# Rooms for the weights' rests 4,224 bytes apart, and the moving parts of every product at one place modulo 256

## The chip, the cores and the metric

The kernel runs on one core of a Trainium2 chip. The metric is the device time of one execution in microseconds. Three runs of the kernel before took 1249.85 us at the median (1249.78 to 1250.2). The profile is one further execution of the same program.

## The reference

Two pre-norm residual layers over 512 tokens of width 1024, in float32. Layer 0 mixes tokens with a grouped complex diagonal state-space model (S5) and a GLU, layer 1 with forgetting attention (FoX, 16 heads of 64). Each is followed by a gated feed-forward with a causal depthwise convolution of width 3 (inner width 2816). A conditioning vector gives shift, scale and gate of every sub-layer. Cut to what the change touches:

```python
def modulate(x, g, shift, scale):
    return rmsnorm(x, g) * (1.0 + scale) + shift

def s5_mixer(h, w_in, ..., w_glu, w_out):
    u = h @ w_in
    ...                                    # scan over the tokens, gelu
    y = y * jax.nn.sigmoid(y @ w_glu)
    return y @ w_out

def fox_mixer(h, w_in, b_f, w_out):
    proj = h @ w_in                        # q, k, v and the forget logits
    ...
    return o @ w_out

def conv_ffn(h, w_up, conv_w, conv_b, w_down):
    a, b = jnp.split(h @ w_up, 2, axis=-1)
    ...                                    # causal convolution of a, width 3
    return (jax.nn.silu(a_conv) * b) @ w_down
```

## The kernel before, in words

**Products in three matmuls.** All activations lie transposed, channels on the 128 partitions and the 512 tokens along the free axis. A float32 weight tile is loaded (line 190, the tile `raw`) and split: ScalarE writes its rounded part `w_hi` (line 275), VectorE the rest `w_lo` = raw - w_hi (line 276). Activations are split in the same way: `a_hi` and `a_lo` for a normed input, `zhi`/`zlo` for the gated S5 output, `ghi`/`glo` for the gated inner layer, and the two halves `o[:, 0]`, `o[:, 1]` of the tile `v` for the attention output. For each of the 8 (or 5 or 6) slices of the contraction, `mms` (line 287) issues three matmuls on line 292: (`w_hi`, `x_hi`), (`w_hi`, `x_lo`), (`w_lo`, `x_hi`). The first of each pair is stationary (loaded by LDWEIGHTS), the second is the moving part, which streams 512 tokens of 4 bytes, or 256 in a half.

**Stages in order of time.** S5 runs up to 199 us with its float32 inputs and the first four columns of the GLU product (line 1190, `glu_head`); the rest of GLU and `w_out` follow up to 268. The first feed-forward (`ffn`, two groups of 11 inner tiles: up, down, up, down) runs up to about 650. Then come FoX: its values (line 1328, where the weights are the moving part and the input is stationary), the queries and keys with the attention worked in between (lines 1424, 1454, 1471), and `w_out` from about 836 to 893. The second feed-forward, with `plain` set, has four groups; most of its up product is formed from quarter matrices in seven products in place of eight (`quarters`, line 548; `forms_x` prepares the moving parts).

**Rings.** Weights live in the pool `wpool`: `raw` with 3 buffers, `w_hi` and `w_lo` with 5 each (`WB`). In the opening the three rings take turns for raw loads as well (`raw(..., n)`, line 185: n = 2 takes a `w_lo` buffer). The tile framework orders the instructions of each engine ahead of time and gives each new tile a buffer of its ring that has come free; a write waits for the last reader of the tile that had the buffer. In the program as built the buffers of `w_lo` are taken in one fixed turn.

**Places.** The free-axis addresses follow from the sizes of the pools. `a_hi` starts at byte 20,288 of each partition. `ROOM` enlarges the rooms of `a_hi` and `a_lo` by so many floats, and `WHOLE`, `HALF`, `PLAIN` say at which float the content starts (`normed`, line 130). `gap` (line 134) allocates a few floats that only shift what follows. `TAIL_OFF` and `DOWN_OFF` shift the weights inside wider rooms for the tail of a down product and for the other down products (line 628). Slices are 512 or 2,048 bytes, so a tile's place modulo 256 is the same for all its slices.

Of the kernel before, what the change touches and what calls it, by code (L numbers as in the profile page):

```python
# [8 lines left out]
F32 = mybir.dt.float32  # L9
F32R = mybir.dt.float32r  # L10
# [7 lines left out]
P = 128  # L18
D = 1024
KT = D // P  # L20
# [16 lines left out]
HALVES = (slice(0, S // 2), slice(S // 2, S))  # L37
RAW, WB = 3, 5

ROOM = {"a_hi": 112, "a_lo": 80}  # L40
WHOLE = {"a_hi": 0, "a_lo": 48}
HALF = {"a_hi": 112, "a_lo": 0}
PLAIN = {"a_lo": 16}
TAIL_ROOM = 7 * P
TAIL_OFF = {"w_hi": 80, "w_lo": 112}, {"w_hi": 96, "w_lo": 0}
DOWN_OFF = {"w_hi": 0, "w_lo": 96}

GROUPS = (11, 11)
QGROUPS = (6, 5, 6, 5)
# [14 lines left out]
class Trunk:  # L64
# [6 lines left out]
    def __init__(self, tc, io, ctx):  # L71
        self.tc, self.nc, self.io, self.ctx = tc, tc.nc, io, ctx
        nc = self.nc
        pool = lambda name, bufs, **k: ctx.enter_context(tc.tile_pool(name=name, bufs=bufs, **k))
        self.const = pool("const", 1)
        self.act = pool("act", 1)
        self.wpool = pool("wpool", 3)
        self.tmp = pool("tmp", 2)
        self.small = pool("small", 2)
        self.dram = pool("dram", 1, space=DRAM)  # L80
        self.mm = pool("mm", 4, space=PSUM)
        self.aux = pool("aux", 4, space=PSUM)
        self.bg = []
        self.acc = None
        self.pending = None
        self.spaced = False
# [12 lines left out]
        self.ga = [self.const.tile([P, KT], F32, name=f"ga{i}") for i in range(4)]  # L99
# [83 lines left out]
            yield  # L183

    def raw(self, shape, src, n=0):
        if n == 2 and not self.spaced:
            self.spaced = True
            self.gap(self.wpool, 32, "w_gap")
        t = self.wpool.tile(shape, F32, name="raw", tag=("raw", "w_hi", "w_lo")[n], bufs=(RAW, WB, WB)[n])
        self.nc.sync.dma_start(t, src)  # L190
        return t

    def ada_pe(self, i, thirds, late=False):

# [66 lines left out]
    def split(self, src, shape, pool=None, bufs=WB, off=None):  # L261

        if off:
            more = TAIL_ROOM - math.prod(shape[1:])
            hi, lo = (
                self.wide(pool or self.wpool, n, {"bufs": bufs}, F32R, more, off[n], shape) for n in ("w_hi", "w_lo")
            )
        else:
            hi, lo = ((pool or self.wpool).tile(shape, F32R, name=n, bufs=bufs) for n in ("w_hi", "w_lo"))
        self.put_parts(hi, lo, self.raw(shape, src))  # L270
        return hi, lo

# [20 lines left out]
                o, wt, xt[:, cols], start=(k == 0 and n == 0), stop=(k == nk - 1 and n == 2),  # L293
            )

    def product(self, w, ms, nk, x, evac, head=0, tail=0, after=None, ticks=0, halves=HALVES, tail_pool=(), first=None, step=None, apart=False, where=()):


        ms = list(ms)
        full = slice(0, S)  # L300
        if head:
            wk = first or {m: self.weights(w[m], nk) for m in ms[:head]}
# [9 lines left out]
                evac(m, ps[m], full)  # L312
                self.tick(ticks)
        for m in ms[head:len(ms) - tail]:
            wk = self.weights(w[m], nk, *where)
            ps = self.mm.tile([P, S], F32, name="mmp")
            for c in HALVES if apart else (full,):
                for k in range(nk):
                    self.mms(ps[:, c], wk, x, k, nk, c)
                    if step:  # L320
                        step()
            evac(m, ps, full)
            self.tick(ticks)
        if tail:
            last = ms[len(ms) - tail:]
# [184 lines left out]
    def quarters(self, pool, l, f, x, finish):  # L510

        nc = self.nc
        H, N = KT // 2, S // 2
# [5 lines left out]
        w = {}  # L519

        def parts(src, names, where=None):
            hi, lo = where or (
                self.wpool.tile([P, len(names) * H, P], F32R, name=n, bufs=WB) for n in ("w_hi", "w_lo")
            )
            self.put_parts(hi, lo, src)
            for j, n in enumerate(names):
                w[n] = hi[:, j * H:(j + 1) * H], lo[:, j * H:(j + 1) * H]
# [51 lines left out]
    def ffn(self, i, l, x, nxt, ticks=0, plain=None):  # L579

        nc, tc = self.nc, self.tc
        with tc.tile_pool(name=f"ffn{l}", bufs=1, reuse_waits="tile") as pool:
# [17 lines left out]
            def gated(m, ps, cols):  # L600
# [18 lines left out]
                self.put_parts(hi[:, j, :], lo[:, j, :], t)  # L619

            after, y = nxt
            up = lambda fs, **k: self.product(
                self.io["w_up"][l], range(2 * fs[0], 2 * fs[-1] + 2), KT, x, gated, ticks=ticks, **k
            )
            last = len(groups) - 1
            down = lambda q, ms, **k: self.product(
                self.io["w_down"][l][:, :, first[q]:first[q + 1], :], ms, groups[q], g[q],
                self.add_residual(i, q == last), after=after, ticks=ticks, where=(None, WB, DOWN_OFF), **k
            )
            todo = []  # L630
            for q, n in enumerate(groups):
# [146 lines left out]
class S5(Trunk):  # L778
# [291 lines left out]
    def s5(self, i, nxt):  # L1070
# [5 lines left out]
        with ExitStack() as stack:  # L1076
# [3 lines left out]
            with ExitStack() as start:  # L1080
# [12 lines left out]
                with tc.manual_schedule(engines={ENG.PE, ENG.Activation, ENG.DVE, ENG.SP}):  # L1093
# [18 lines left out]
                    rb = self.rms_rows(y, NB)  # L1112
                    next(params)
                    next(scale)
                    x = self.normed("a_lo", PLAIN, "a_x", F32)
                    for k in range(KT):
                        nc.vector.scalar_tensor_tensor(
                            x[:, k], self.h[:, k], self.ga[i][:, k:k + 1], rb, op0=ALU.mult, op1=ALU.mult
# [62 lines left out]
            def glu_head(k, part):  # L1181

                for m in range(HEAD):
                    if part and m not in lo:
                        lo[m] = self.wpool.tile([P, KT, P], F32R, name="w_lo", bufs=WB)
                        with tc.issue_after(self.scanned):
                            nc.vector.tensor_tensor(lo[m], raw[m], hi[m].bitcast(F32), ALU.subtract)
                    wt = (hi, lo)[part][m][:, k]
                    for xt in (yhi, ylo) if part == 0 else (yhi,):
                        nc.tensor.matmul(  # L1190
                            gps[m], wt, xt[:, k], start=(k == 0 and part == 0 and xt is yhi), stop=(k == KT - 1 and part == 1)
                        )
# [69 lines left out]
class Kernel(S5):  # L1262
# [320 lines left out]
```

## Time and profile before

| | before |
|---|---|
| median of three runs | 1249.85 us |
| the profiled execution's own time | 1250.39 us |
| its span, first to last instruction | 1248.6 us |
| TensorE busy with matmuls | 1225.7 us, 98% |
| VectorE, ScalarE, GpSimd busy | 896.8, 565.0, 57.6 us |
| mean granted TensorE clock | 0.994 |

The span and what lies around it (1.8 us) make the execution's own time, which is 0.54 us above the median of the runs. Matmuls are pipelined: the duration of one matmul overlaps the next, so a rate is read from how many matmuls a stretch of the chain holds and not from the duration of one. In a row of the chain of waits the first number is the start in us, the second the length in us, and "x174" the number of instructions that the row joins.

### The profile page before, as it was taken

Reading aid. Unit: us, or ns where it says so; the run is one execution under the profiler, and the core shown is the slowest. Engines: PE = TensorE matmul, PEld = TensorE weight load, DVE = VectorE, ACT = ScalarE, POOL = GpSimd, SP = SyncE. Lnnn points to the kernel's source line nnn. Section 1 sums busy time; section 2 is a strip of 40 time slices with the busy share of each in tenths; the row PEclk is TensorE's granted clock in tenths of the full one; section 3 lists DMA queues with packets and bytes.
Section 4 is the critical chain, followed back from the end, with each engine's and each line's share of the span. In section 5 each row is a group of like instructions: output and inputs, shape, how many; then the busy total and the mean of one; then the engine's idle time right before and its main releaser. Section 6 shows DMA issues by size and latency. Waiting matters only on the chain.

```text
span 1248.6 us, 19613 instructions
## 1 busy us (share of the span) xinstructions
PE 1225.7 (98%) x7584; PEld 1021.2 (82%) x7584; DVE 896.8 (72%) x1610; ACT 565.0 (45%) x1043; POOL 57.6 (5%) x111
## 2 busy tenths in 40 slices
PE   7999999999999999999999999999989999999997
PEld 2466677898778887787799888887989999999987
DVE  7888886479755546566457467765799978888865
ACT  3543455335333223333434366664456555555543
POOL 0000000000000000000000143331000000000000
PEclk9999999999999999999999999999999999999999
DMA  9678667336735746455423343240413332333331
GB/s 360 229 237 261 201 185 255 104 104 208 247 125 164 221 140 220 136 173 162 142 70 101 127 133 132 95 144 5 133 38 116 114 115 92 110 108 106 102 85 69
DMA packets 73068, 183.24 MB, mean 147 GB/s; under 512 B 23079, under 2 KB 25471, under 8 KB 71951
## 3 DMA queue, kind: packets, MB, share of 16 engines
q1 hardware_dynamic: 72687, 181.46, 45.0%
q8 instruction: 60, 0.98, 0.3%
q10 hardware_dynamic: 288, 0.52, 0.1%
q14 instruction: 33, 0.27, 0.1%
HBM read 175.04 MB, written 6.92 MB: 146 GB/s over the span
## 4 chain that ended last, share of the span: by engine, by line
PE 94%; DVE 3%; ACT 1%; DMA 1%; issue 1%; SPq 0%; DVEq 0%; ACTq 0%
PE mmp L292 57%; PE mmp L548 10%; PE mmp L1161 4%; PE aux L548 4%; PE mmp L1328 2%; PE aux L966 2%; PE mmp L1190 2%; PE aux L1471 2%; PE aux L1454 1%; PE mmp L209 1%; PE aux L1055 1%; PE aux L1047 1%; PE aux L1424 1%; PE mmp L1101 1%; PE aux L1005 1%; DVE w_lo L276 1%
## 5 line engine op out<-in xcount | busy, mean ns | idle before, releaser
L275 ACT ACTIVATE w_hi<-raw 128x1024 fp32r<-128x1024 f32 (+4 forms) x197 | 181.1, 926 | 257.5 <-PE mmp L292 211.0
L276 DVE TENSOR_TENSOR w_lo<-raw,w_hi 128x1024 fp32r<-128x1024 f32 (+4 forms) x197 | 210.1, 1068 | 90.4 <-ACT w_hi L275 86.1
L292 PE MATMUL mmp<-a_hi,w_hi 128*128 128x512 f32 (+1 forms) x664 | 244.3, 369 | 1.5 <-ACT a_hi L429 0.8
L292 PE MATMUL mmp<-a_hi,w_lo 128*128 128x512 f32 (+1 forms) x664 | 240.8, 363 | 3.1 <-DVE w_lo L276 3.1
L292 PE MATMUL mmp<-a_lo,w_hi 128*128 128x512 f32 (+1 forms) x664 | 241.6, 365 | 0.0
L292 PEld LDWEIGHTS mmp<-a_hi,w_hi 128*128 128x128 f32 x664 | 125.2, 189 | 25.7 <-issue 2.6
L292 PEld LDWEIGHTS mmp<-a_hi,w_lo 128*128 128x128 f32 x664 | 125.2, 189 | 24.5 <-DVE w_lo L276 3.3
L292 PE MATMUL mmp<-ghi,w_hi 128*128 128x512 f32 (+1 forms) x394 | 144.6, 367 | 0.0
L292 PE MATMUL mmp<-glo,w_hi 128*128 128x512 f32 (+1 forms) x394 | 144.1, 366 | 0.0
L292 PE MATMUL mmp<-ghi,w_lo 128*128 128x512 f32 (+1 forms) x394 | 144.0, 365 | 0.0
L292 PEld LDWEIGHTS mmp<-a_lo,w_hi 128*128 128x128 f32 x664 | 125.4, 189 | 18.6
L359 DVE SCALAR_TENSOR_TENSOR h<-mmp,par,h 128x512 f32<-128x512 f32 (+1 forms) x74 | 49.9, 676 | 58.0 <-PE mmp L292 57.7
L292 PEld LDWEIGHTS mmp<-ghi,w_lo 128*128 128x128 f32 x394 | 74.0, 188 | 12.2
L292 PEld LDWEIGHTS mmp<-ghi,w_hi 128*128 128x128 f32 x394 | 74.0, 188 | 11.6
L292 PEld LDWEIGHTS mmp<-glo,w_hi 128*128 128x128 f32 x394 | 74.0, 188 | 11.5
L237 DVE SCALAR_TENSOR_TENSOR ada_acc<-ada_raw,sc,ada_acc 128x1024 f32<-128x1024 f32 x49 | 62.8, 1282 | 27.9 <-DMA ada_raw<-in_ada_w 27.6
L548 PE MATMUL mmp<-w_hi 128*128 128x256 f32 x216 | 59.7, 277 | 0.0
L548 PE MATMUL mmp<-w_lo,w_hi 128*128 128x256 f32 x216 | 59.6, 276 | 0.0
L548 PE MATMUL mmp<-w_hi,w_lo 128*128 128x256 f32 x216 | 59.6, 276 | 0.0
L609 ACT ACTIVATE conv<-conv 128x512 f32<-128x512 f32 x44 | 27.6, 631 | 64.2 <-DVE conv L606 63.8
L1161 PE MATMUL mmp<-a_x,raw 128*128 128x512 f32 x112 | 56.2, 640 | 0.0
L276 DVE TENSOR_TENSOR w_lo<-sums,w_hi 128x1024 fp32r<-128x1024 f32 x40 | 48.5, 1221 | 3.3 <-ACT w_hi L275 2.1
(306 smaller groups left out, 2479.6 us busy)
## 6 DMA issues: line engine op xcount, KB each, us to landing
raw<-in_w_up SPq DMA_DIRECT2D x88, 512.0 KB, 3.3
ada_raw<-in_ada_w SPq DMA_DIRECT2D x56, 512.0 KB, 4.4
raw<-in_ada_w SPq DMA_DIRECT2D x40, 512.0 KB, 6.1
raw<-in_w_down SPq DMA_DIRECT2D x32, 384.0 KB, 3.2
raw<-in_w_down SPq DMA_DIRECT2D x32, 320.0 KB, 3.0
nf<-nfd SPq DMA_DIRECT2D x8, 1152.0 KB, 5.7
raw<-in_fox_qk SPq DMA_DIRECT2D x16, 512.0 KB, 3.6
h<-in_x SPq DMA_DIRECT2D x8, 512.0 KB, 5.2
```

Of the source, the lines that this page charges most:

```text
L237: nc.vector.scalar_tensor_tensor(acc, w, self.sc[:, k:k + 1], acc, op0=ALU.mult, op1=ALU.add)
L275: nc.scalar.activation(hi, src, AF.Copy)
L276: nc.vector.tensor_tensor(lo, src, hi.bitcast(F32), ALU.subtract)
L292: self.last_mm = self.nc.tensor.matmul(o, wt, xt[:, cols], start=(k == 0 and n == 0), stop=(k == nk - 1 and n == 2),)
L359: self.nc.vector.scalar_tensor_tensor(self.h[:, m, cols], ps, self.par[i][:, 16 + m:17 + m], self.h[:, m, cols], op0=ALU.mult, op1=ALU.add,)
L548: self.last_mm = nc.tensor.matmul(o, wt[:, k], xt[:, k], start=(first and k == 0 and n == 0), stop=(k == H - 1 and n == 2), skip_group_che ...
L609: nc.scalar.activation(t, t, AF.Silu)
L966: nc.tensor.matmul(ps[g2][:, j, cols], x[rows, a + j, r].rearrange("p c j -> p (c j)"), self.rr[rows, planes, q, :], start=(j == 0 and r = ...
L1161: nc.tensor.matmul(ps, w[m][:, k, :], x[:, k], start=(k == 0), stop=(k == KT - 1))
L1190: nc.tensor.matmul(gps[m], wt, xt[:, k], start=(k == 0 and part == 0 and xt is yhi), stop=(k == KT - 1 and part == 1))
L1328: self.last_mm = nc.tensor.matmul(ps[q, b][:, :n], xt[:, k, tb], wt, start=(k == 0 and i == 0), stop=(k == KT - 1 and i == 2),)
L1471: nc.tensor.matmul(pv[:, c * P:], self.v[:, hp, k, r].rearrange("p t d -> p (t d)"), pp[:, r, c + 3 * k:NB + 3 * k, :].rearrange("p b t -> ...
```

## The change

- `w_lo` is no longer one ring of five buffers. `rest` hands out five rooms, each a tag of its own with one buffer, in a fixed turn by a counter (`self.rests`). A room is 32 floats wider than the largest content, 4,224 bytes, so that the rooms start 0, 128, 0, 128, 0 bytes off modulo 256; the content starts 0 or 128 bytes in, by the room's number, or the other way round with `odd`. So all rests lie at one place modulo 256, and with `odd` all lie 128 bytes further.
- `odd` is set for the up products of the second feed-forward (`up` with `plain`, and `quarters`), not elsewhere. `DOWN_OFF` and `where` go, and with them the shifted rest of the down products; `w_gap`, which stood ahead of the `w_lo` ring, goes too.
- `ROOM`, `WHOLE`, `HALF` change, `PLAIN` goes; `zlo_gap` goes, and `v_gap` shrinks from 48 to 32 floats.

Worked out from the sizes: `a_hi` at 20,288 is 4,096 + 48 floats, so `a_lo` starts at 36,864 and is 4,096 + 16 floats; `wpool` starts at 53,312, `raw` and `w_hi` take eight times 4,096 bytes, and the rooms start at 86,080 and end at 107,200. The `w_lo` ring ended at 107,200 as well, so what follows in memory stays where it was, but for the tiles after the two changed gaps. Places modulo 256, in bytes:

| tile | before | after |
|---|---|---|
| `raw`, `w_hi` | 64 | 64 |
| `w_lo` and raw loads in its place | 192 | 64 |
| `w_lo` of the down products | 64 | 64 |
| `w_lo` of the second feed-forward's up products | 192 | 192 |
| `a_hi`, whole / for the second feed-forward | 64 / 0 | 64 / 0 |
| `a_lo`, whole / for the second feed-forward | 192 / 0 | 64 / 0 |
| `zhi`, `zlo` | 64, 192 | 64, 64 |
| `v` (and `o`), `phi`, `plo`, q and k parts | 128 | 64 |
| `ghi`, `glo` | 64 | 64 |
| weights of the down tails, hi / lo | 128 / 0 | 128 / 0 |
| moving parts of `quarters` | 0 | 0 |

Modulo 512 the picture differs: `a_hi` lies at 320 before and after, `a_lo` at 448 before and at 64 after, and the five rests (not `odd`) at 64, 320, 320, 64, 64.

```diff
-ROOM = {"a_hi": 112, "a_lo": 80}
-WHOLE = {"a_hi": 0, "a_lo": 48}
-HALF = {"a_hi": 112, "a_lo": 0}
-PLAIN = {"a_lo": 16}
+ROOM = {"a_hi": 48, "a_lo": 16}
+WHOLE = {"a_hi": 0, "a_lo": 16}
+HALF = {"a_hi": 48, "a_lo": 0}
 TAIL_ROOM = 7 * P
 TAIL_OFF = {"w_hi": 80, "w_lo": 112}, {"w_hi": 96, "w_lo": 0}
-DOWN_OFF = {"w_hi": 0, "w_lo": 96}
...
     def raw(self, shape, src, n=0):
-        if n == 2 and not self.spaced:
-            self.spaced = True
-            self.gap(self.wpool, 32, "w_gap")
-        t = self.wpool.tile(shape, F32, name="raw", tag=("raw", "w_hi", "w_lo")[n], bufs=(RAW, WB, WB)[n])
+        if n == 2:
+            t = self.rest(shape, F32, "raw")
+        else:
+            t = self.wpool.tile(shape, F32, name="raw", tag=("raw", "w_hi")[n], bufs=(RAW, WB)[n])
         self.nc.sync.dma_start(t, src)
         return t
+
+    def rest(self, shape, dt=F32R, name="w_lo", odd=False):
+
+        i = self.rests % WB
+        self.rests += 1
+        n = math.prod(shape[1:])
+        t = self.wpool.tile([P, n + 32], dt, name=name, tag=f"w_lo{i}", bufs=1)
+        a = 32 * ((i + odd) % 2)
+        t = t[:, a:a + n]
+        return t.rearrange("p (a b) -> p a b", b=shape[2]) if len(shape) == 3 else t
...
         else:
-            hi, lo = ((pool or self.wpool).tile(shape, F32R, name=n, bufs=bufs) for n in ("w_hi", "w_lo"))
+            hi = self.wpool.tile(shape, F32R, name="w_hi", bufs=WB)
+            lo = self.rest(shape, odd=self.odd)
...
-            wk = self.weights(w[m], nk, *where)
+            wk = self.weights(w[m], nk)
...
-            hi, lo = where or (
-                self.wpool.tile([P, len(names) * H, P], F32R, name=n, bufs=WB) for n in ("w_hi", "w_lo")
-            )
+            shape = [P, len(names) * H, P]
+            hi, lo = where or (self.wpool.tile(shape, F32R, name="w_hi", bufs=WB), self.rest(shape, odd=True))
...
-            up = lambda fs, **k: self.product(
-                self.io["w_up"][l], range(2 * fs[0], 2 * fs[-1] + 2), KT, x, gated, ticks=ticks, **k
-            )
+            def up(fs, **k):
+                self.odd = bool(plain)
+                self.product(self.io["w_up"][l], range(2 * fs[0], 2 * fs[-1] + 2), KT, x, gated, ticks=ticks, **k)
+                self.odd = False
...
-                self.add_residual(i, q == last), after=after, ticks=ticks, where=(None, WB, DOWN_OFF), **k
+                self.add_residual(i, q == last), after=after, ticks=ticks, **k
...
-                    x = self.normed("a_lo", PLAIN, "a_x", F32)
+                    x = self.normed("a_lo", WHOLE, "a_x", F32)
...
-                        lo[m] = self.wpool.tile([P, KT, P], F32R, name="w_lo", bufs=WB)
+                        lo[m] = self.rest([P, KT, P])
...
             zhi = pool.tile([P, KT, S], F32R, name="zhi")
-            self.gap(pool, 32, "zlo_gap")
             zlo = pool.tile([P, KT, S], F32R, name="zlo")
...
-            self.gap(pool, 48, "v_gap")
+            self.gap(pool, 32, "v_gap")
```

More of the change, by code (lines that the diff above doesn't have):

```diff
@@ L85, in __init__ @@
         self.pending = None
-        self.spaced = False
+        self.rests, self.odd = 0, False
         self.ones = self.const.tile([P, P], F32, name="ones")
@@ L264, in split @@
             more = TAIL_ROOM - math.prod(shape[1:])
-            hi, lo = (
-                self.wide(pool or self.wpool, n, {"bufs": bufs}, F32R, more, off[n], shape) for n in ("w_hi", "w_lo")
-            )
-        else:
-            hi, lo = ((pool or self.wpool).tile(shape, F32R, name=n, bufs=bufs) for n in ("w_hi", "w_lo"))
+            hi, lo = (self.wide(pool, n, {"bufs": bufs}, F32R, more, off[n], shape) for n in ("w_hi", "w_lo"))
+        elif pool:
+            hi, lo = (pool.tile(shape, F32R, name=n, bufs=bufs) for n in ("w_hi", "w_lo"))
+        else:
+            hi = self.wpool.tile(shape, F32R, name="w_hi", bufs=WB)
+            lo = self.rest(shape, odd=self.odd)
         self.put_parts(hi, lo, self.raw(shape, src))
@@ L294, in mms, with product @@
             )
-    def product(self, w, ms, nk, x, evac, head=0, tail=0, after=None, ticks=0, halves=HALVES, tail_pool=(), first=None, step=None, apart=False, where=()):
+    def product(self, w, ms, nk, x, evac, head=0, tail=0, after=None, ticks=0, halves=HALVES, tail_pool=(), first=None, step=None, apart=False):
         ms = list(ms)
@@ L621, in ffn @@
             after, y = nxt
-            up = lambda fs, **k: self.product(
-                self.io["w_up"][l], range(2 * fs[0], 2 * fs[-1] + 2), KT, x, gated, ticks=ticks, **k
-            )
+            def up(fs, **k):
+                self.odd = bool(plain)
+                self.product(self.io["w_up"][l], range(2 * fs[0], 2 * fs[-1] + 2), KT, x, gated, ticks=ticks, **k)
+                self.odd = False
             last = len(groups) - 1
```

## The prediction

> **What bounds the kernel now.** I read the page first, then the waits of TensorE, then the chain of waits in short windows inside single stages, then the groups by shape. From the page, engines and chain:
>
> ```profile
> PE 1225.7 (98%) x7584; PEld 1021.2 (82%) x7584; DVE 896.8 (72%) x1610; ACT 565.0 (45%) x1043; POOL 57.6 (5%) x111
> PE 94%; DVE 3%; ACT 1%; DMA 1%; issue 1%; SPq 0%; DVEq 0%; ACTq 0%
> ```
>
> The waits of TensorE, those that matter here (line, releaser: us in total, times, longest):
>
> ```profile
> PE mmp L292 <- DVE w_lo L276: 3.1, 1, 3.1
> PE mmp L292 <- ACT a_hi L429: 0.8, 1, 0.8
> PE mmp L1328 <- DVE v L276: 0.4, 1, 0.4
> PE mmp L209 <- DMA raw<-in_ada_w: 0.2, 1, 0.2
> ```
>
> TensorE bounds the kernel almost everywhere; a nanosecond off each matmul is a nanosecond off the end. So the question is the spacing of matmuls of one form. Windows of the chain, each inside one stage (start us, length us, matmuls):
>
> ```profile
> 319.84 40.22 PE mmp L292 x174
> 419.81 36.27 PE mmp L292 x160
> 221.89 31.20 PE mmp L292 x135
> 864.09 16.13 PE mmp L292 x69
> 687.96 10.14 PE mmp L1328 x86
> 952.51 3.51 PE mmp L548 x31
> ```
>
> Length by count gives the spacing. The first two are the up and the down product of the first feed-forward: 231.1 and 226.7 ns, both with 512 moving columns. The third, S5's `w_out`, 231.1. The fourth, FoX's `w_out`, 233.8 (69 matmuls, so good to one in 69, some 3 ns). The last two have 256 columns: FoX's values 117.9, the second feed-forward's quarters 113.2. The clock was the same in up and down, and all of both windows was matmul (us; PE busy, PEld busy, clock, DMA share, GB/s):
>
> ```profile
> 320.00:360.00 40.00, 40.00 (x175) 32.49 (x174) 1.00 0.57 185
> 420.00:460.00 40.00, 40.00 (x178) 33.10 (x177) 1.00 0.63 206
> ```
>
> So the slow one is not slower by the clock or by more DMA traffic. What differs is the place. With the table of places: the fast down product has both moving parts at 64 and both weights at 64. The fast quarters have moving parts all at 0, weights at 64 and 192. The slow up product, S5's `w_out` and the values have parts that change between 64 and 192 from one matmul to the next. FoX's `w_out` is slow with both parts at one place, 128: being at one place is not enough by itself, and the exact place seems to count. After the change it stands at 64, the place of the fast down product.
>
> **The change part by part.** The number of matmuls that come from a slow place to the fast one, from the groups by shape (a group is one of the three matmuls of a slice):
>
> ```profile
> L292 PE MATMUL mmp<-a_hi,w_hi 128*128 128x512 f32 x488 | 195.0, 400 | 0.7 <-ACT nm_t L1250 0.7
> L292 PE MATMUL mmp<-ghi,w_hi 128*128 128x512 f32 x310 | 121.0, 390 | 0.0
> L292 PE MATMUL mmp<-zlo,w_hi 128*128 128x512 f32 x48 | 19.0, 395 | 0.0
> L292 PE MATMUL mmp<-v,w_lo 128*128 128x512 f32 x48 | 18.9, 393 | 0.0
> L1190 PE MATMUL mmp<-a_hi,w_hi 128*128 128x512 f32 x32 | 12.7, 401 | 0.0
> L292 PE MATMUL mmp<-a_hi,w_hi 128*128 128x256 f32 x176 | 49.4, 285 | 0.8 <-ACT a_hi L429 0.8
> L292 PE MATMUL mmp<-zhi,w_hi 128*128 128x256 f32 x32 | 9.1, 286 | 0.0
> L292 PE MATMUL mmp<-v,w_lo 128*128 128x256 f32 x32 | 9.0, 281 | 0.0
> L1328 PE MATMUL mmp<-w_hi,a_hi 128*128 128x256 f32 x96 | 27.0, 285 | 0.4 <-DVE v L276 0.4
> L1328 PE MATMUL mmp<-w_hi,a_hi 128*128 128x272 f32 x16 | 4.7, 295 | 0.0
> L1471 PE MATMUL aux<-phi,v 128*128 128x256 f32 x32 | 8.3, 282 | 0.0
> ```
>
> With 231.1 - 226.7 = 4.4 ns for a full matmul off the 64/192 pair and 117.9 - 113.2 = 4.7 for a half:
>
> - up, GLU, and queries and keys, 3 x 488 = 1,464 x 4.4 = 6.44 us;
> - S5's `w_out`, 144 x 4.4 = 0.63; the GLU heads of line 1190, 96 x 4.4 = 0.42;
> - FoX's `w_out`, 144 x (233.8 - 226.7) = 1.02;
> - halves: of the 176 groups 128 belong to the second feed-forward, which keeps its places; the heads of the first have 3 columns x 8 slices x 2 halves = 48 groups, 144 matmuls x 4.7 = 0.68; S5's tail 96 x 4.7 = 0.45; FoX's tail 96 x 4.7 = 0.45;
> - values, 288 x 4.7 = 1.35; those of 272 columns start at four places in turn, so half of it, 96 x 2.4 = 0.23;
> - the weighing by `phi` and `plo` (line 1471), 128 matmuls that come from 128 to 64: between nothing and 128 x 4.4 = 0.56, as no row has them at 64; I take 0.28.
>
> Together 11.95 us. The down products (3 x 310 matmuls of the `ghi` row), the tails and the second feed-forward keep their places modulo 256 and should not move; the float32 matmuls of the opening change only where their weights stand, and I give that nothing.
>
> What is lost again. TensorE waits where the row of waits shows it at a norm: 0.8 us for `a_hi`. The first halves of the heads run ahead of that wait, and what they gain (half of 0.68) is waited out: 0.3. At the second feed-forward's start, with the 3.1 us for `w_lo`, VectorE sets the pace; FoX's tail starts that work earlier, but its last quarter only covers it: 0.2. In the values VectorE is filled by the splits and by the forget logits, and TensorE waits 0.4 us for `v` already; of the 1.6 us that the values gain I take 0.8 as waited out (between 0 and 1.6). Of VectorE, and the chain in that place:
>
> ```profile
> 670.86 1.23 DVE L276 TENSOR_TENSOR w_lo<-raw,w_hi 128x1024 fp32r<-128x1024 f32 x1 [0.94 <-ACT w_hi L275]
> 673.06 1.23 DVE L276 TENSOR_TENSOR w_lo<-raw,w_hi 128x1024 fp32r<-128x1024 f32 x1 [0.98 <-ACT w_hi L275]
> 674.93 0.42 DVE L276 TENSOR_TENSOR v<-aux,v 128x256 fp32r<-128x256 f32 x1 [0.64 <-ACT v L275]
> 674.10 0.39 PE aux L1328 x3
> ```
>
> Here the five fixed rooms add a wait. The first five rests are all read to the end of the first values, at 674.5. Before, a new rest takes whichever buffer comes free; now it takes the room next in turn, and the one written at 673.06 would take the room of the third rest, which holds the last slices. It would start at 674.5: 1.4 us late, with the evictions of `v` and the forget logits queued behind it on VectorE, and TensorE behind the evictions. The 0.64 us of idle time ahead of the next eviction takes part of it up, so 0 to 0.8 us; I take 0.4. Elsewhere the ring already goes round in one turn, and fixed rooms change nothing; in the opening SyncE's loads into rooms would be the ones held, and the row of 0.2 us is all that TensorE waits for such a load (were one late by its whole trip, 6 us by the page's 6.1 to landing).
>
> ```profile
> raw<-in_ada_w SPq DMA_DIRECT2D x40, 512.0 KB, 6.1
> L276 DVE TENSOR_TENSOR w_lo<-raw,w_hi 128x1024 fp32r<-128x1024 f32 x112 | 138.5, 1238 | 63.6 <-ACT w_hi L275 59.5 <-PE mmp L1190 2.1
> L276 DVE TENSOR_TENSOR w_lo<-raw,w_hi 128x768 fp32r<-128x768 f32 x32 | 30.5, 954 | 21.3 <-ACT w_hi L275 21.2
> L276 DVE TENSOR_TENSOR w_lo<-raw,w_hi 128x640 fp32r<-128x640 f32 x32 | 26.2, 820 | 3.0 <-ACT w_hi L275 2.9
> ```
>
> VectorE's subtraction writes to another place now, raw, `w_hi` and rest all at 64. The down rests did so before: from 640 to 768 elements 134 ns, so 1,024 at 64 would take 954 + 268 = 1,222 ns against 1,238 at 192. No cost. The removed gaps are small fills on GpSimd, 5% busy.
>
> Losses 0.3 + 0.2 + 0.8 + 0.4 = 1.7 us. Net 11.95 - 1.7 = 10.25: the profiled execution's 1250.39 us would be 1240.1. It stands 0.54 above the median of the runs, so the median would be 1239.6 us.
>
> [...]
>
> **The rivals.**
>
> First, the place counts modulo 512. Then `a_hi` at 320 and `a_lo` at 64 still change from matmul to matmul and up, GLU, queries and values keep their spacing (6.44 + 0.42 + 0.68 + 1.58 stay away). What remains is S5's `w_out`, FoX's `w_out` and the weighing: 0.63 + 0.45 + 1.02 + 0.45 + 0.28 = 2.8, less 0.2 and 0.4 of the losses: 1249.85 - 2.2 = 1247.6 us. Against it: the down product stands at 64 modulo 512 in the first feed-forward and its moving parts at 320 in the second, with weights at 64 in both; for it, no stretch of the profile alternates by 256.
>
> Second, the place is not the cause. Up differs from down in more than place (tiles of 8 against 5 and 6 slices, other work on ScalarE and VectorE), and FoX's `w_out` is slow at one place. Then nothing moves but the added wait in the values: 1249.85 + 0.4 = 1250.3 us. Against it: the quarters share the up product's weights and neighbours and go at 113.2.
>
> Third, slower: the price grows with the distance between consecutive places, and modulo 512 at that. Today's 128 bytes cost 4.4 ns per full matmul; 256 bytes between `a_hi` and `a_lo` would cost 8.8, so the up row's 1,464 lose 6.4 us instead of gaining them, the GLU heads 0.4, the heads of the first feed-forward 0.7; the values, whose rests alternate in two rooms of five, 0.6. That is 8.1; less the 2.2 that the first rival keeps net: 1249.85 + 5.9 = 1255.8 us. It decides only if 256 bytes apart is not the same place; against it speaks the pair of down products again.
>
> **How the numbers follow.** The forecast has 0.76, the first rival 0.09, the second 0.07, the third 0.06; 0.02 stay for an order of instructions that the framework lays out otherwise. The forecast's own range: with no losses and the weighing whole, 1249.85 - 12.2 = 1237.6; with losses at their upper ends (0.3 + 0.2 + 1.6 + 0.8 = 2.9), no gain of the weighing and FoX's `w_out` by 4.4 only, 1249.85 - 11.3 + 2.9 = 1241.5, and with one matmul of 135 miscounted in the windows (1.7 ns on some 2,000) 3 us more, 1244.9. To leave out no more than 2 in 10 it reaches to the first rival: 1237.5 to 1248.0. About 0.2%, 2.5 us, is what a measurement of this kernel can tell from no change. Faster by more than that holds the forecast and a part of the rest, 0.79; within it, most of the first and all of the second rival, 0.14; slower, the third and a part of the rest, 0.07.
>
> **What would show it.** In the profile after, the windows of up, S5's `w_out` and FoX's `w_out` should go at 226 to 228 ns and the values at 113 to 114; the down product and the quarters should stay at 226.7 and 113.2. If up stays at 231 while S5's `w_out` drops, the first rival holds; if none drops, the second; if up goes to 235, the third. The added wait would show as a longer wait of the values for `v`, and as VectorE waiting for line 1328. The forecast is wrong outright if a window at 64/64 stays above 229.

## The result, and the profile after

The changed kernel takes 1245.41 us at the median of 12 runs (1243.1 to 1249.75), the kernel before, run beside it, 1250.87 us (1247.77 to 1254.84): 5.5 us less, a ratio of 0.9956 with a 95% interval of 0.9942 to 0.9969. A second series later, of the same two programs, gave 1244.76 us against 1251.51, a ratio of 0.9949 (0.9933 to 0.9966). So the change makes the kernel faster by some 6 us. The direction is as forecast and the time lies in the range, but beyond the likeliest case's own range, which ended at 1244.9, and a gain of 10.25 us, as forecast, lies outside both intervals.

From the page of the changed kernel, its engines and the head of its chain:

```profile
PE 1221.6 (98%) x7584; PEld 1023.6 (82%) x7584; DVE 896.0 (72%) x1610; ACT 564.9 (45%) x1043; POOL 57.1 (5%) x109
PE 93%; DVE 2%; DMA 2%; issue 1%; ACT 1%; SPq 0%; DVEq 0%; ACTq 0%
```

TensorE bounds it as before. The order of all transfers is the same in both programs, and so is that of the 7,584 matmuls but for twelve in FoX's values, so each matmul can be set beside its counterpart. (Line 301 of the changed kernel is line 292 of the one before, 1337 is 1328, 556 is 548, 285 is 276, 1259 is 1250.) The chain of waits of the changed kernel in windows inside single stages, start us, length us, matmuls:

```profile
324.89 30.15 PE mmp L301 x133
415.93 36.29 PE mmp L301 x160
221.97 31.08 PE mmp L301 x137
863.88 12.13 PE mmp L301 x53
949.48 3.63 PE mmp L556 x32
256.92 4.08 PE mmp L301 x34
272.98 5.04 PE mmp L301 x42
686.94 7.08 PE mmp L1337 x59
699.88 11.10 PE mmp L301 x49
717.90 1.39 PE mmp L301 x6
719.94 2.06 PE mmp L301 x9
```

Length by count gives the spacing, in ns from the start of one matmul to the start of the next. Up now goes at 226.7 ns, as down does (226.8), and S5's `w_out` at 226.9. FoX's `w_out` is at 228.9 and the quarters at 113.4. So far the forecast. But the next three rows, all of 256 columns, are at 120.0: S5's tail, the heads of the first feed-forward and the values. The last three rows are queries and keys: 226.5 in one long stretch, 231.7 and 228.9 in the short ones between pieces of attention. The kernel before had, in the same places (S5's tail, the heads, queries and keys):

```profile
256.94 2.59 PE mmp L292 x22
272.94 3.18 PE mmp L292 x27
700.00 12.03 PE mmp L292 x52
```

That is 117.7, 117.8 and 231.3 ns. The half-wide matmuls became slower where 4.7 ns less was forecast. The waits of TensorE in the changed kernel's profile that bear on the forecast:

```profile
PE mmp L301 <- DVE w_lo L285: 3.1, 1, 3.1
PE mmp L301 <- ACT nm_t L1259: 1.8, 1, 1.8
PE mmp L301 <- ACT a_hi L438: 0.8, 1, 0.8
```

The waits for `w_lo` and `a_hi` are unchanged and that of the values for `v` is gone. New is 1.1 us at the start of the S5 GLU (1.8 instead of 0.7), for a transfer that landed late: in the chain there the `raw` of `in_s_w_glu` takes 8.89 us, where the median of the eight is 4.8. The experiments below, the same program again among them, have 0.7 there, so it is of that execution and not of the change. Of VectorE's waits between 640 and 700 us, where the values stand, one is new:

```profile
DVE w_lo L285 <- PE aux L1337: 3.7, 2, 2.0
```

It is the sign that the prediction gave for the added wait of a rest for its fixed room (line 1337 was 1328). VectorE has this wait, but TensorE doesn't wait for `v` behind it.

The spacings over whole stages are start to start of consecutive matmuls of one form, without those more than a fifth above the rest. "Measured" is what the starts of the same matmuls differ by in the two profiles, added up over the term, so it is not just the count times the difference of the spacings; for the GLU product the late transfer and the half clock behind it are left out.

| term | forecast, us | spacing before, after, ns | measured, us |
|---|---|---|---|
| up (984) | -4.33 | 231.1, 226.9 | -4.14 |
| GLU product (96) | -0.42 | 231.2, 226.9 | -0.35 |
| queries and keys (384) | -1.69 | 231.4, 229.5 | -0.61 |
| S5's `w_out` (144) | -0.63 | 231.1, 226.9 | -0.58 |
| GLU heads (96) | -0.42 | 230.7, 227.6 | -0.28 |
| FoX's `w_out` (144) | -1.02 | 232, 228 | -0.45 |
| heads of the first feed-forward (144) | -0.68 | 117.7, 119.9 | +0.30 |
| S5's tail (96) | -0.45 | 117.6, 119.7 | +0.16 |
| FoX's tail (96) | -0.45 | 118.9, 119.8 | +0.09 |
| values (288 and 96) | -1.58 | 117.7, 119.6 | -0.17 with the wait for `v` |
| weighing | -0.28 | 232.1, 227.8 at 512 | -0.23 |
| sum | -11.95 | | -6.3 |
| losses | +1.7 | | none seen |

The measured sum lies between the two differences of the medians, 5.5 and 6.75 us. The two profiled executions themselves differ by only 3.2 us (1250.39 and 1247.16): in that of the changed kernel the opening took 0.8 us more, the late transfer 1.1, and 1.3 went in the GLU product behind it, where the clock stood at 0.50 for 3.4 us.

### The profile page after: what moved, and what is told of

It reads as the page before. It is cut to its first block, busy times and chain, and to the rows that moved or that the text cites. A ratio compares the mean times of both kernels' runs of the same rounds, so it can differ in the third digit from the quotient of the medians.

```text
span 1245.4 us, 19609 instructions
## 1 busy us (share of the span) xinstructions
PE 1221.6 (98%) x7584; PEld 1023.6 (82%) x7584; DVE 896.0 (72%) x1610; ACT 564.9 (45%) x1043; POOL 57.1 (5%) x109
## 4 chain that ended last, share of the span: by engine, by line
PE 93%; DVE 2%; DMA 2%; issue 1%; ACT 1%; SPq 0%; DVEq 0%; ACTq 0%
PE mmp L301 57%; PE mmp L556 10%; PE mmp L1171 4%; PE aux L556 4%; PE mmp L1337 3%; PE aux L976 2%; PE aux L1480 2%; PE aux L1463 1%; PE mmp L217 1%; PE aux L1057 1%; PE aux L1065 1%; PE aux L1433 1%; PE mmp L1111 1%; PE aux L1015 1%; DMA raw<-in_s_w_glu 1%
```

## The experiments

Executions of one program differ by up to 8 us (1241.2 to 1249.27 in twelve runs of the changed kernel). The first eight experiments ran once each, so their times decide little and they are read by their spacings. The first four take the two sides apart: where the moving parts stand and where the weights stand. A pair such as "64/192" gives the places of hi and lo modulo 256.

**Rests at 192.**

```diff
-                self.odd = bool(plain)
+                self.odd = True
```

> Only the rests (w_lo) of the first feed-forward's up product go to 192; w_hi and both moving parts stay at 64. Theory M (the moving parts' place alone decides): up stays at 226.9 ns and the time within 0.3 us of the changed kernel; its heads of 256 columns stay at 119.9. Theory W (a product of 512 columns is fast only where both weights stand with the moving parts): the 984 matmuls of up go back towards 231, so the second up product is 2 to 4 us later. Theory O (for 256 columns the weights must stand 64 away from the moving parts): heads go from 119.9 to about 117, as one of three now stands off. The wait of the S5 GLU for nm_t: 0.7 us if the 1.8 us of the changed kernel's profile was a late transfer of that run, 1.8 if the change causes it.

Measured 1247.32 us. Up in the chain:

```profile
324.89 30.28 PE mmp L301 x131
```

That is 231.1 ns, all of the old price, with both moving parts still at 64. S5's `w_out`, left as it was, has 226.8. So the moving parts' place does not decide alone: theory M falls, and this run is as W says. The heads come to 119.0, not 117: O's size is wrong for this arrangement. The wait for `nm_t` is 0.7 us.

**a_hi at 192.**

```diff
-WHOLE = {"a_hi": 0, "a_lo": 16}
+WHOLE = {"a_hi": 32, "a_lo": 16}
```

> Only a_hi moves, to 192, with a_lo at 64 and all weights at 64: the moving parts of every product that reads a change between 64 and 192 again, as before the change. Theory M: up, GLU and queries and keys go back to 231 (about 6 us in all), S5's w_out and FoX's w_out stay at 226.9 and 228. Rival R (the equal place of the weights was what counted, w_hi and w_lo both at 64): up stays at 226.9. Theory O: the heads of 256 columns come to about 117 (a mean of 113 off the weights' place and 120 on it).

Measured 1247.53 us. Up:

```profile
324.82 30.21 PE mmp L301 x132
```

228.9 ns, half way between M's 231 and R's 226.9, so neither is right. With the first experiment: the weights' change of place alone costs 4.3 ns, the moving parts' alone 2.0, and both together no more than 4.2 (the kernel before). The prices don't add.

**Moving parts at 0, weights at 64/192.**

```diff
-WHOLE = {"a_hi": 0, "a_lo": 16}
+WHOLE = {"a_hi": 48, "a_lo": 0}
-                self.odd = bool(plain)
+                self.odd = True
...
-                        lo[m] = self.rest([P, KT, P])
+                        lo[m] = self.rest([P, KT, P], odd=True)
...
+            self.odd = True
             self.product(self.io["s5_w_glu"], range(HEAD, KT), KT, (yhi, ylo), glu)
+            self.odd = False
...
+        self.odd = True
         self.product(self.io["fox_qk"], range(NH), KT, x, project, step=self.unit)
+        self.odd = False
```

> a_hi and a_lo both at 0, and the rests of up, GLU, its heads and queries and keys at 192 with w_hi at 64: the places of the second feed-forward, whose 256 columns take 113.2 ns. Theory O: full matmuls keep 226.9, the heads of the first feed-forward go from 119.9 to 113.2 (144 x 6.7 ns = 1.0 us), the values, with a as the weights at 0 and w moving at 64, from 119.6 to 113 (288 x 6.6 = 1.9 us, part of it waited out for v); 1 to 2.5 us faster than the changed kernel. Theory M: full matmuls 226.9, half ones 120, no change of time. Theory W (full matmuls are fast only with weights and moving parts at one place): up, GLU and queries and keys at 229 or more, 3 to 6 us slower.

Measured 1250.8 us, no faster than the kernel before (1250.23 beside it). This kernel's chain misses these stages, so here are the first and last of 174 matmuls of up on the timeline, and of 46 of the heads:

```profile
319.79 0.40 PE L301 MATMUL mmp<-a_hi,w_lo 128*128 128x512 f32 x1
...
359.90 0.39 PE L301 MATMUL mmp<-a_lo,w_hi 128*128 128x512 f32 x1
...
279.77 0.28 PE L301 MATMUL mmp<-a_hi,w_lo 128*128 128x256 f32 x1
...
284.91 0.28 PE L301 MATMUL mmp<-a_hi,w_lo 128*128 128x256 f32 x1
```

40.11 us over 173 intervals is 231.8 ns for the full matmul, and 5.14 over 45 is 114.2 for the half one, in one arrangement. The two widths want opposite things. The full matmul is slow off the moving parts' place (231.8), as W says; the half matmul is fast off it (114.2), as O says. The values, with 64 moving over weights at 0/0, come to 117.7, not to O's 113.

**z and v at 0, weights at 64/192.**

```diff
-            self.gap(pool, 32, "z_gap")
+            self.gap(pool, 16, "z_gap")
...
+            self.odd = True
             self.product(self.io["s5_w_out"], range(KT), KT, (zhi, zlo), self.add_residual(i), tail=2, after=after)
+            self.odd = False
...
-            self.gap(pool, 32, "v_gap")
+            self.gap(pool, 16, "v_gap")
...
+            self.odd = True
             self.product(
                 self.io["fox_w_out"], range(KT), KT, lambda k: (self.o[k][:, 0], self.o[k][:, 1]),
                 self.add_residual(i), head=4, tail=2, after=after,
                 halves=(slice(0, S),), step=self.unit,
             )
+            self.odd = False
```

> zhi, zlo and v (also the o made in it), phi, plo and the queries and keys stand at 0 instead of 64, rests of S5's w_out and FoX's w_out at 192: S5's tail, FoX's tail and all of the attention's own matmuls change, a and its products don't. Theory O: S5's and FoX's tails go from 119.7 to 113.2 (192 x 6.5 ns = 1.2 us), scores and weighing, whose two sides both go to 0, stay as they are; full ones at 226.9. Theory M: nothing changes by more than 0.3 us. Theory W: the 288 full matmuls of S5's and FoX's w_out go to 229 to 231, 0.6 to 1.2 us slower.

Measured 1246.34 us. S5's `w_out` and its tail:

```profile
221.77 28.28 PE mmp L301 x122
256.89 3.17 PE mmp L301 x28
```

231.8 ns for the full columns, 113.2 for the tail's half ones, and FoX's pair the same (231.7, 114.5). It repeats the third experiment in other tiles, with up untouched at 226.9. Here the two effects nearly cancel in each of the two stages: 0.7 us lost on 144 matmuls, 0.5 won on 96.

**Moving parts at 0, weights all at 64.** Is it a change of place that costs, or a difference of place?

```diff
-WHOLE = {"a_hi": 0, "a_lo": 16}
+WHOLE = {"a_hi": 48, "a_lo": 0}
```

> a_hi and a_lo at 0 as in e3_a_at_0, but every weight of its products stays at 64, so the weights don't alternate. Theory E (a full matmul is at its fastest only where moving parts and weights stand at the very same place modulo 256): up stays slow, 229 to 232 as in e3. Theory C (what costs is a change of place from one matmul to the next, of the weights or of the moving part): nothing changes place, up goes at 226.9 and the time is that of the changed kernel. Halves: the heads at 113.3 if it is enough that the weights stand off the moving place; 117.6 if they must stand to both sides of it, as 117.6 is what the values of e3 show with 64 moving over 0.

Measured 1252.9 us (the kernel before beside it: 1253.48). Up, and two windows of the heads:

```profile
324.97 30.10 PE mmp L301 x129
271.93 5.89 PE mmp L301 x50
280.97 6.12 PE mmp L301 x54
```

Nothing changes place from one matmul to the next, and up takes 233.3 ns, the slowest of all. Theory C falls and E holds as far as places were tried: the full matmul is at its fastest where moving parts and weights stand at the very same place, here 64 (226.9). The heads show 117.8 in the first window and 113.3 in the second, at the same places. With the weights to one side only, both spacings occur; which of them comes is not explained by these runs.

**a_hi at 128, a_lo at 0.**

```diff
-WHOLE = {"a_hi": 0, "a_lo": 16}
+WHOLE = {"a_hi": 16, "a_lo": 0}
```

> a_hi at 128, a_lo at 0, all weights at 64. In the values, where a is the weights and w moves at 64, that is the arrangement of the down tails (moving 64, weights 128 and 0), which take 113.6 ns. Theory B (a half matmul is fast where its two weights stand to the two sides of the moving place): the values go from 119.6 to 113.6, 288 x 6 ns = 1.7 us, if no wait for v takes it; rival: they stay at 117 to 120, and the values are slow for another reason, such as their order. Up, GLU and queries and keys move at 128 and 0 over 64: by theory E and by theory C slow, 229 to 232, 984 x 2 to 5 ns = 2 to 5 us later after up.

Measured 1246.43 us. Up and the values in the chain:

```profile
324.78 30.41 PE mmp L301 x132
687.92 7.14 PE mmp L1337 x63
```

And the wait of the values, from TensorE's waits between 640 and 700 us:

```profile
PE mmp L1337 <- DVE v L285: 0.6, 1, 0.6
```

The values, moving at 64 over weights at 128/0, go at 113.3 ns in this window and 115.0 over the stage. Theory B holds for them, and their order isn't to blame. But standing to both sides is not enough. FoX's tail in the kernel before, moving at 128 over 64/192, had its weights to both sides as well and was slow, 118.7 ns in the chain:

```profile
883.89 2.73 PE mmp L292 x23
```

There `w_hi` stood 64 bytes below the moving place and `w_lo` 64 above; in the fast cases it is the other way round. Whether that is the reason, no run shows.

Of the 1.3 us that 288 x 4.6 ns would bring, the stage as a whole gained 0.6 against the changed kernel: the wait for `v` came back with 0.6. Up is slow, 230.4, as E has it.

**Up cut into runs of six.** Why do queries and keys keep 229.5 at the places where up goes at 226.9?

```diff
+    def blip(self, n=1):
+        self.blips = getattr(self, "blips", 0) + 1
+        if self.blips % 2 == 0:
+            t = self.aux.tile([P, S], F32, name="aux")
+            self.nc.tensor.transpose(t[:, :P], self.ident, self.ident)
...
-                self.product(self.io["w_up"][l], range(2 * fs[0], 2 * fs[-1] + 2), KT, x, gated, ticks=ticks, **k)
+                self.product(self.io["w_up"][l], range(2 * fs[0], 2 * fs[-1] + 2), KT, x, gated, ticks=ticks, step=None if plain else self.blip, **k)
```

> The changed kernel with one 128-column transpose of a constant put into the first feed-forward's up product after every second slice, so that its full matmuls come in runs of six, as those of the queries and keys come between pieces of attention. The added transposes leave an unused tile; they cost their own time, some 160 times 0.1 us or less, which isn't the question. Theory S (the fast spacing is reached only some ten matmuls after an interruption): up's full matmuls take 229 to 231 within their runs, as the queries' 229.5. Rival N (queries and keys are slower because of the other work of their stage on ScalarE and VectorE): up stays at 226.9.

Measured 1267.33 us. The chain in up, one transpose between each two runs (line 307 is line 301 here):

```profile
330.96 1.39 PE mmp L307 x6
332.36 0.11 PE aux L187
332.47 1.40 PE mmp L307 x6
333.86 0.11 PE aux L187
```

1.39 us for six is 232 ns, with the interval up to the transpose; inside the runs, without the longer first interval, the mean of 656 is 230.8 instead of 226.9. Places and neighbouring work are up's own, so the interruption by another matmul is enough: theory S holds and N falls. The 164 transposes and the slower spacing cost some 20 us (1267.33 against 1245.41).

**Queries and keys in longer runs.**

```diff
                 self.attend(pool, m // 2, qp.pop(m // 2), (hi, lo), nfd)
+            self.unit(KT)
...
-        self.product(self.io["fox_qk"], range(NH), KT, x, project, step=self.unit)
+        self.product(self.io["fox_qk"], range(NH), KT, x, project)
```

> The changed kernel with the pieces of attention taken in after each column of queries or keys (24 full matmuls) and not after each slice (3). Theory S: from the tenth matmul of a run on 226.7 ns, all of the stage's full matmuls at 227.5 to 228. Rival N: 229.5 as now, at whatever position. The pieces of one column now follow each other without matmuls between them, so TensorE waits for the softmax more, and the time is some us or tens of us longer; that isn't the question.

Measured 1256.39 us. The mean over the stage is 228.8 ns, above the 227.5 to 228 expected, since many runs still were of 8 or 15 matmuls. By position in a run it is as S says, though not a smooth fall: 234.2, 231.5, 234.2, 227.1, 229.3 and 231.9 for the second to seventh interval of a run (22 runs), 227.6, 229.4 and 228.3 for the eighth to tenth (15 runs), and 226.3 to 227.0 from the eleventh to the end of the column. In the chain, nine matmuls at the start of a run and the last ten of a run of 24, 232.2 and 227.0 ns:

```profile
742.57 2.09 PE mmp L301 x9
754.78 2.27 PE mmp L301 x10
```

The work of ScalarE and VectorE in that stage takes nothing from the settled spacing that shows: 226.3 to 227.0 there, 226.9 in up.

**The same program again, and a wait filled.** The executions of one program differ by more than some of the terms. One place was seen to differ from run to run: behind TensorE's wait of 3.1 us at the second feed-forward.

```diff
+                        if f == 3:
+                            ps = self.aux.tile([P, S], F32, name="aux")
+                            for _ in range(22):
+                                nc.tensor.matmul(ps[:, :S // 2], x[0][:, 0, :P], x[0][:, 0, :S // 2], start=True, stop=True)
                         if f > 1:
                             up([f], apart=True)
```

> The changed kernel itself once more, as the measure for the two beside it. Its spacings repeat to 0.2 ns (up 226.9, S5's w_out 226.9, queries and keys 229.5, values 119.6). If the late transfer ahead of the S5 GLU was of one run, TensorE waits 0.7 us for nm_t this time, as in all experiments so far, not 1.8. After the wait of 3.1 us for w_lo at the second feed-forward, the clock stands at 0.50 for a time that differs by run (nothing in e1 and e6, 15 matmuls of 213 ns in the kernel before, 30 in e4): between 0 and 3.3 us.

> The changed kernel with 22 matmuls of 256 columns into an unused tile ahead of the two columns in whose midst TensorE waits 3.1 us for w_lo; order of everything else as before. They take 22 x 113 ns = 2.5 us of that wait. Theory G (after this wait the clock is halved for up to 3.3 us, in some runs not at all, and that is most of the scatter between runs): the wait shrinks to 0.6 us, the clock stays at 1.00 behind it, the median falls by 0.7 to 1.7 us against e9 and the runs lie closer together. Rival: the clock doesn't depend on this wait, and the time is that of e9, within 0.3 us.

Measured 1244.76 us (1241.2 to 1249.27, 12 runs) for the same program and 1245.14 (1241.67 to 1248.58, 12 runs) for the filled wait. One microsecond soon after that wait as a window, first of the changed kernel's first profile, then of the same program again (stretch, length; busy PE, PEld, DVE, ACT, POOL with counts; clock, DMA share, GB/s):

```profile
931.00:932.00 1.00, 1.00 (x7) 1.00 (x6) 1.00 (x2) 0.00 (x0) 0.00 (x0) 0.50 0.99 389
```

```profile
930.00:931.00 1.00, 1.00 (x7) 1.00 (x7) 1.00 (x3) 0.00 (x0) 0.00 (x0) 0.50 0.72 291
```

Of the filled wait the same window, and one of the opening:

```profile
931.00:932.00 1.00, 0.99 (x8) 1.00 (x9) 1.00 (x1) 0.00 (x0) 0.00 (x0) 1.00 0.10 12
72.00:76.00 4.00, 4.00 (x11) 2.31 (x11) 2.55 (x4) 3.98 (x15) 0.00 (x0) 0.50 0.08 29
```

Its waits of TensorE that bear on this:

```profile
PE mmp L556 <- ACT nm_h L563: 0.6, 2, 0.3
PE mmp L301 <- DVE w_lo L285: 0.5, 1, 0.5
```

Behind the unfilled wait the clock is at 0.50 and the matmuls start 214 ns apart, so that only seven reach into a microsecond where eleven do at 1.00: for 15 matmuls in the first profile, for 25 in the second, and in the first and the sixth experiment not at all. With the wait filled to 0.5 us the clock stays at 1.00 (926 to 928 and 930 to 934 us); in the last experiment, which has the filled wait too (0.4 us), no slice of the page shows a clock below 0.9. Over twelve runs each the mean granted clock is 0.995 against 0.993. What makes the clock fall is not shown: in the first profile 3.4 us lie between the starts of the two matmuls around the wait, and behind the same wait of 3.1 us the clock fell in some executions and not in others.

But the time didn't fall. In its profile the filled wait gained 2.65 us up to the 5,400th matmul against the same program again, and gave 1.4 back by the 5,700th in the quarters, which now wait for the evictions of line 563 (0.6 us of it stands in the row of `nm_h`, which the same program again does not have). What remained doesn't show in the medians. Nor did the scatter go: 6.9 us between lowest and highest run, 8.1 without. It goes with the clock: of the twelve runs of the same program the fastest, 1241.2 us, has a mean granted clock of 0.996 and the slowest, 1249.27 us, of 0.990. The window of the opening shows where more of it is: this execution, the slowest of its twelve, ran from 72 to 76 us at half clock, where the same program again had 1.00, and lost 4.6 us to it between the 300th and the 400th matmul. On the clock the windows agree with theory G but don't show it, as in two of the six profiles with the wait unfilled (the kernel before, the changed one, and the first, fourth, sixth and ninth experiments) the clock stayed at 1.00 too. On the time it is wrong.

**S5's tail with weights to both sides.** On top of the filled wait:

```diff
+S5_OFF = {"w_hi": 16, "w_lo": 48}
...
-            more = TAIL_ROOM - math.prod(shape[1:])
+            more = 64 if off is S5_OFF else TAIL_ROOM - math.prod(shape[1:])
...
-            self.product(self.io["s5_w_out"], range(KT), KT, (zhi, zlo), self.add_residual(i), tail=2, after=after)
+            self.product(self.io["s5_w_out"], range(KT), KT, (zhi, zlo), self.add_residual(i), tail=2, after=after, tail_pool=(pool, 2, S5_OFF))
```

> e10 and the two last columns of S5's w_out with weights in tiles of their own, w_hi at 128 and w_lo at 0 over moving parts at 64, as in the down tails. Theory B: their 96 matmuls of 256 columns go from 119.7 to 113.6, 0.6 us less, and with the filled wait some 2 us less than e9. If the place to both sides was not what makes the down tails fast, they stay at 119.7 and the time is that of e10.

Measured 1243.38 us (1239.84 to 1244.68, 6 runs), a ratio of 0.9929 to the kernel before (0.9905 to 0.9954). S5's tail in the chain (line 302 is line 301):

```profile
256.99 3.06 PE mmp L302 x27
```

113.3 ns, moving at 64 over 128/0, with the full columns at 226.9: theory B holds here too, with `w_hi` above and `w_lo` below once more. The median is the lowest of all, 1.4 us below the same program again, but the two intervals overlap, so that it beats the changed kernel is not shown. The heads of the first feed-forward and FoX's tail, 240 matmuls x 6 ns = 1.4 us (119.9 and 119.8 against 113.3 to 114.1), should gain in the same way, by this estimate; it wasn't tried.

## Why the prediction was right, and where it was wrong

**The pair of windows, 231.1 against 226.7.** Right, and right that modulo 256 is what counts: `a_hi` stands at 320 and `a_lo` at 64, and up goes at 226.9. The first rival (modulo 512), the second (place is not the cause) and the third (a price growing with distance) fall together. Up, GLU product and S5's `w_out` gained 5.07 of the 5.38 us forecast. Place alone moved up between 226.9 (the changed kernel) and 233.3 (the fifth experiment).

**"What differs is the place", read as alternation.** The prediction took moving parts that alternate for the cause and the weights along with them. The fifth experiment has no alternation, and up is the slowest of all there. What counts for a full matmul, in all arrangements tried, is that moving parts and weights stand at one place: 226.7 to 227.1 there where no other matmul cuts in, 228.9 to 233.8 elsewhere. For up this made no difference, since the change brings both about.

**The halves, 4.7 ns less: the step that failed.** The prediction carried the fast half, 113.2 in the quarters, over to 64/64 on both sides. But the quarters move at 0 over 64/192, and the down tails at 64 over 128/0: in both `w_hi` stands 64 bytes above the moving place and `w_lo` 64 below. The third, fourth, sixth and last experiments brought slow halves into this arrangement, and they went at 113 to 115 ns. The change set both weights at the moving place instead, and there halves are slow, 119.8. In place of 3.16 us gained (1.58 in heads and tails, 1.58 in the values) stand 0.55 lost and 0.17 gained. The table of places had it: no half matmul of the kernel before was fast at one place, and the two widths should not have been given one rule. Of this difference 3.5 us come.

**Queries and keys by up's price.** Wrong in size: 0.61 of 1.69 us. The place is right, but the stage is cut into runs of 3 to 15 matmuls, and the first ten of a run don't yet go at 226.7 (227.1 to 234.2 by position in the eighth experiment). The long windows taken as the measure had no interruption in them. By the prediction's own mark, a window at 64/64 above 229, it would be wrong outright in these runs (231.7), but the seventh and eighth experiments show the interruption and not the place as the reason. The same holds for the first half of FoX's `w_out`, which attention also cuts: 229.1 there, not 226.7.

**FoX's `w_out` at 233.8.** Mis-sized: 0.45 us came and not 1.02. The window of 69 lay in the last 72 matmuls of full width, and for these it was right: 233.8 before, 227.1 after. The first 72, which attention cuts into runs of 3 to 12, went at 230.0 and came only to 229.1. The value of the uncut half was taken for the whole stage.

**The losses, 1.7 us.** None showed. The waits for `a_hi` and `w_lo` are what they were (0.8 and 3.1), and the heads didn't run ahead, as they were not faster. The values' waits of 0.8 and 0.4 stayed away with their gain: the wait for `v` vanished when they became slower and came back, with 0.6 us, as soon as the sixth experiment made them fast. That the values' gain would be waited out in part was right. The fixed rooms did hold VectorE, 3.7 us in two waits for line 1337, but cost TensorE nothing there: no wait for `v` is left in the changed kernel.

So of 4.0 us between the 10.25 forecast and the 6.3 of the spacings, 3.5 are the halves and values, 1.1 queries and keys, 0.6 FoX's `w_out`, 0.4 the small terms of full matmuls, the GLU heads among them, and 0.1 the weighing, together 5.7; the 1.7 of losses that did not come stand against them.

## What to carry to other kernels

Where TensorE's spacing sets the time, read it from windows of one form and one stage, and compare it for each width and each length of run by itself; a spacing read in one arrangement need not hold in another, as full matmuls here went from 226.9 to 233.8 ns by arrangement. For matmuls of 512 columns try first moving parts and both weights at one place modulo 256 bytes, which gave 226.9 ns here (at 64), and for those of 256 `w_hi` 64 bytes above the moving place and `w_lo` 64 below, which gave 113.2 to 115.0 (moving parts at 0 and at 64). Interleaving small pieces of other work on TensorE cost more here than the pieces: inside runs of six, full matmuls came at 230.8 instead of 226.9 ns, and in longer runs the intervals up to the tenth took 227.1 to 234.2, those after it 226.3 to 227.0.

## What the runs showed of the hardware that was not expected

The arrangements side by side, spacing in ns at full clock (mean over a stage, places of hi/lo modulo 256):

| moving | weights | 512 columns | 256 columns | from |
|---|---|---|---|---|
| 64/192 | 64/192 | 231.1 | 117.7 | the kernel before |
| 128/128 | 64/192 | 233.8 where uncut | 118.9 | the kernel before, FoX's `w_out` |
| 64/64 | 64/64 | 226.9 | 119.8 | the changed kernel |
| 64/64 | 64/192 | 231.2 | 119.0 | first |
| 192/64 | 64/64 | 228.9 | 119.5 | second |
| 0/0 | 64/192 | 231.8 | 114.4 | third, fourth |
| 0/0 | 64/64 | 233.3 | 117.8, then 113.3 | fifth |
| 128/0 | 64/64 | 230.4 | 117.4 | sixth |
| 64/64 | 0/0 | | 117.7 in the values | third |
| 64/64 | 128/0 | | 115.0 in the values, 114.1 in S5's tail | sixth, last |

Two things are new. The arrangement that is best for the full width (226.9) is the worst for the half one (119.8), and that in which the half one goes at 114.4 has the full one among its slow ones (231.8). And the fast spacing took some ten matmuls to settle in the eighth experiment: 227.1 to 234.2 by position up to the tenth interval of a run, 226.3 to 227.0 from the eleventh. Why the prices of two alternating sides don't add, why FoX's tail was slow with its weights to both sides in the kernel before, and why the fifth experiment's heads go through two spacings at the same places, stays open; what in the chip reads by these places is not shown by any run here.
